# Stick-breaking attention: the first 512 keys of each unit multiplied on GpSimd and turned by TensorE in the score bank, the later keys by DMA

## The chip, the cores and the metric

The kernel runs on one core of one Trainium2 chip. The metric is device time in microseconds (us), from the first to the last instruction of one execution, as the median of several runs. Five engines work side by side, each through its own queue in order: TensorE (PE; its weight loads are shown as PEld), VectorE (DVE), ScalarE (ACT), GpSimd (POOL) and SyncE (SP), which here issues nearly all transfers to the DMA engines. SBUF is the working memory of 128 partitions; PSUM holds the matmul results in banks of 128 x 512 float32.

## What is computed

One layer of a streaming encoder with two kinds of attention heads side by side, on 2048 positions of width 1024. Cut to what matters here, the stick-breaking half:

```python
def one_block(args):                      # 128 queries of 8 heads, width 64
    qb, blk = args
    q_pos = blk * QBLK + jnp.arange(QBLK)
    z = jnp.einsum('bqhd,bkhd->bhqk', qb, k) * scale
    mask = (k_pos[None, :] < q_pos[:, None])[None, None]
    log_1mb = jnp.where(mask, jax.nn.log_sigmoid(-z), 0.0)
    rem = lax.cumsum(log_1mb, axis=3, reverse=True) - log_1mb
    a = jnp.where(mask, jnp.exp(jax.nn.log_sigmoid(z) + rem), 0.0)
    return jnp.einsum('bhqk,bkhd->bqhd', a, v)
```

So the weight of a key is sigmoid(z) times the product of sigmoid(-z) over the keys between it and the query. Ahead of it stand an RMS norm and one projection to q, k, v of both kinds of heads; behind it the output projection, a second norm and a gated feed-forward part.

## The kernel before

**Stages.** There are 8 groups of heads: groups 0 to 3 are one differential head each, groups 4 to 7 two stick-breaking heads each (`m` is 0 or 1). While a group's attention runs, the projection of the next group is woven in; under group 7 the output projection is woven in instead. The feed-forward part follows and takes the second half of the time. The order in each engine's queue is set when the kernel is built: the code yields work in pieces, a scheduler places the instructions by priorities (`PRI`) and its own costs, and `tc.issue_after(x)` keeps an instruction behind another one. On the chip each queue then runs in that order and waits where it must.

**A unit of stick-breaking** is one block `i` of 128 queries, one head `m` and up to 1024 keys (`b` counts these from the last); a group has 48 of them. `stage_a` treats a unit in chunks of 512 keys, the later chunk (`c` = 1) first, then `c` = 0. A group has 48 chunks with `c` = 0 and 32 with `c` = 1, 80 in all. For a chunk:

- TensorE makes the scores into a PSUM bank `sc` (`score_chunk`, L507; three products in half precision with high and low halves for groups 4 to 6, where `turned(g)` is true, and two for group 7). Four such banks go round in turn, so a chunk's bank is wanted again four chunks later.
- ScalarE makes sigmoid(-z) into `om` (L619) and sigmoid(z) (L620). VectorE's scan (L622) turns `om` into running products, from the last key to the first.
- The product of sigmoid(z) and the shifted `om` goes into `be` (L623). For groups 4 to 6 the chunk `c` = 1 has its sigmoid(z) in SBUF and GpSimd multiplies; every other chunk has it in the score bank and VectorE multiplies. With that the bank is free.

When both chunks are done, `split_t` splits the unit's whole `be` into high and low half-precision parts in `s16` (named `s` in profiles): the high part by a cast on ScalarE (L89), the low part by a subtraction on GpSimd (L98). One DMA transpose of SyncE (L461) turns both into `aT`, with the keys on the partitions. `PD` + 2 = 7 units later (group 7: 5), `stage_b` has TensorE multiply `aT` with the values (`pv`, L518), and `finish` normalizes a row of blocks; its four transposes are L489. `aT` has 6 buffers, and every fourth unit of groups 4 and 5 takes a spare one of another pool. L342 and L326 are the projections, L832 the output projection, L665 and L683/L684 the transposes of the inputs and their split.

Other numbers: `note` and `pick` keep tallies of each engine's load, by which some casts and subtractions choose an engine.

Of the kernel before, what the change touches and what calls it, by code (L numbers as in the profile page):

```python
# [11 lines left out]
F32 = mybir.dt.float32  # L12
# [26 lines left out]
QB, KB, ZB, AB, SB, PD = 4, 7, 9, 6, 3, 5  # L39
XL = (0, 4, 5, 1, 2, 6, 3)  # L40
# [19 lines left out]
def block(tc, a, out):  # L60
# [3 lines left out]
    with top:  # L64
# [192 lines left out]
        with ExitStack() as ph1:  # L257
# [254 lines left out]
            @pri("pv")  # L512
            def pv(G, yp, y0, aT, b, n, o, wd, start, stop):
                nb = n // P
                for j in range(nb):
                    v = G["v"][2 * b + j // 4][:, j % 4, :]
                    for q, (a_, v_) in enumerate(((j, o), (j, o + wd), (nb + j, o))):
                        PE.matmul(yp[:, y0 : y0 + wd], lhsT=aT[:, a_, :], rhs=v[:, v_ : v_ + wd], start=start and j == 0 and q == 0, stop=stop and j == nb - 1 and q == 2, skip_group_check=True)  # L518
# [77 lines left out]
            def sb_attn(g, G):  # L596
                last = {}
                front = []
                wide = [0]
                lag = PD + 2 if g < NG - 2 else PD  # L600

                @pri("at")
                def stage_a(i, m, b):
# [7 lines left out]
                    last[m] = om  # L611
                    for c in range((n - 1) // 512, -1, -1):
# [4 lines left out]
                        aside = c == 1 and turned(g)  # L617
                        beta = be[:, lo:hi] if aside else sc[:, :w]
# [4 lines left out]
                        (POOL if aside else DVE).tensor_tensor(be[:, lo:hi], beta, om[:, lo + 1 : hi + 1], ALU.mult)  # L623
                        note("A", 1.7 * w + 400)
                        note("D", 2.1 * w + 150)
                        note("P" if aside else "D", (1.65 if aside else 1.05) * w + 100)
                    wide[0] += 1
                    return n, split_t(be[:, :n], n, "A", "P", wide[0] if g < NG - 2 else None)
# [3 lines left out]
                def stage_b(i, m, b, n, aT):  # L632
                    with tc.issue_after(front[-1]):
                        stage_c(i, m, b, n, aT)

                def stage_c(i, m, b, n, aT):
# [4 lines left out]
                    pv(G, yp, P * r + 64 * m, aT, b, n, 128 * m, 64, r == 0 and m == 0 and b == i // 8, r == k - 1 and m == 1 and b == 0)  # L641
# [6 lines left out]
                for i in range(NT):  # L648
                    if i % 4 == 0:
                        level()  # L650
                    for b in range(i // 8, -1, -1):
                        for m in range(2):
                            n, aT = stage_a(i, m, b)
                            pend.append((i, m, b, n, aT))
# [3 lines left out]
                            yield done / (272 + 48 * CS), (i + 1 if b == 0 and m == 1 else i)  # L658
                for u in pend:
# [686 lines left out]
```

## Time and profile before

| | us |
|---|---|
| median of 3 runs | 2679.14 (2677.55 to 2685.42) |
| the profiled execution | 2680.8 |
| busy: TensorE | 2492.4 |
| busy: VectorE | 1932.7 |
| busy: GpSimd | 1489.1 |
| busy: ScalarE | 1347.0 |
| scans of stick-breaking, first and last start | 603.7 and 1353.3 |

The profile is one execution, taken by the hardware profiler; its span is 2680.8 us. A line such as `L622 DVE TENSOR_TENSOR_SCAN z<-z,sc 128x512 ... x168 | 213.5, 1274 | 13.5 <-ACT sc L620 6.0` reads: line 622, on VectorE, writes a tile `z` from `z` and `sc`, 168 times, 213.5 us in all, 1274 ns each on average; before these the engine idled 13.5 us, and 6.0 of that ended when ScalarE's line 620 was done. A line of waits gives the sum, the number and the longest. A line of a stretch gives its busy time for each engine, with the number of instructions, the granted TensorE clock (1.00 is full), the DMA share and rate. Groups that are cut by the edge of a stretch can differ by a call or two from the counts in the code. `om` and `be` are both named `z`.

### The profile page before, as it was taken

The page shows a single profiled execution, that of the slowest core. Times are in us where ns is not written, and L with a number is a line of the kernel's source. Part 1 is how long each engine was busy: PE and PEld are TensorE (multiplying, and loading weights), DVE is VectorE, ACT ScalarE, POOL GpSimd, SP SyncE. Part 2 cuts the span into 40 slices and gives each one's busy share as a digit, 9 for nine tenths or more (in the row PEclk, how much of TensorE's full clock was granted, in tenths as well). Part 3 has the DMA queues.
Part 4 walks back from the last instruction along what each step waited for, and adds up shares of the span by engine and source line. Part 5 has one row for each costly group of instructions (what it writes and reads, how often), then busy time and mean ns, then how long its engine had stood idle before and what let it go on. Part 6 is the DMA issues. An engine that isn't in the chain of part 4 may idle for free. (4 is left out here: it accounts for less than half of the span.)

```text
span 2680.8 us, 50579 instructions
## 1 busy us (share of the span) xinstructions
PE 2492.4 (93%) x19628; PEld 1498.6 (56%) x19628; DVE 1932.7 (72%) x3711; ACT 1347.0 (50%) x2487; POOL 1489.1 (56%) x1098
## 2 busy tenths in 40 slices
PE   6998989888988989889989899999999999999999
PEld 4655656577776776557775344444444444444444
DVE  6898969898989989877766868777685544444434
ACT  4665656567978878665644535344352112111121
POOL 2578667667767766546764656565564232322323
PEclk9999999999999999999999899999999999999999
DMA  6777697767998979987897574665649743635532
GB/s 222 213 162 181 146 200 168 179 143 184 193 179 179 185 160 209 210 191 217 218 285 282 208 250 178 255 226 202 245 183 346 293 177 143 233 141 186 195 111 95
DMA packets 619585, 534.41 MB, mean 199 GB/s; under 512 B 480640, under 2 KB 548224, under 8 KB 609104
## 3 DMA queue, kind: packets, MB, share of 16 engines
q1 hardware_dynamic: 617520, 529.09, 69.9%
q8 instruction: 154, 2.52, 0.4%
q0 software_dynamic: 512, 1.36, 0.2%
q14 instruction: 87, 0.71, 0.1%
q10 hardware_dynamic: 1312, 0.72, 0.1%
HBM read 261.08 MB, written 147.32 MB: 152 GB/s over the span
## 5 line engine op out<-in xcount | busy, mean ns | idle before, releaser
L98 POOL TENSOR_TENSOR s<-z,s 128x1024 f16<-128x1024 f32 (+7 forms) x288 | 472.0, 1647 | 142.5 <-ACT s L89 109.8
L507 PE MATMUL sc<-kT,qT 128*128 128x512 f16 (+3 forms) x1520 | 382.0, 353 | 53.3 <-DVE z L623 19.3
L622 DVE TENSOR_TENSOR_SCAN z<-z,sc 128x512 f32<-128x512 f32 (+3 forms) x320 | 352.8, 1112 | 58.6 <-ACT sc L620 38.0
L1138 PE MATMUL pd<-wd,act 128*128 128x512 f16 x1764 | 390.9, 379 | 1.2 <-DVE cg L1071 1.2
L326 PE MATMUL pj<-w,xt 128*128 128x384 f16 x1920 | 352.2, 331 | 18.8 <-ACT xt L683 6.9
L1030 PEld LDWEIGHTS <-wg 128*128 128x128 f16 x1848 | 182.0, 99 | 230.2 <-issue 16.4
L518 PE MATMUL yp<-v,aT 128*128 128x64 f16 (+1 forms) x4896 | 269.8, 204 | 41.6 <-DMA aT<-s 40.2
L518 PEld LDWEIGHTS <-aT 128*128 128x128 f16 x4896 | 237.5, 99 | 120.4 <-DMA aT<-s 52.5
L1030 PEld LDWEIGHTS <-wu 128*128 128x128 f16 x1848 | 180.7, 98 | 218.0 <-issue 2.6
L98 POOL TENSOR_TENSOR act<-cg,act 128x512 f16<-128x512 f32 x112 | 148.5, 1337 | 262.9 <-ACT act L1097 150.8
L1138 PEld LDWEIGHTS <-act 128*128 128x128 f16 x1764 | 172.8, 98 | 209.4 <-issue 2.8
L326 PEld LDWEIGHTS <-xt 128*128 128x128 f16 x1920 | 187.3, 99 | 147.5 <-issue 21.4
L89 ACT CAST s<-z 128x128 f16<-128x128 f32 (+7 forms) x215 | 173.1, 809 | 134.1 <-DMA aT<-s 40.5
L98 POOL TENSOR_TENSOR hs<-hs,cu 128x512 f32<-128x512 f32 x99 | 130.9, 1328 | 171.3 <-DVE hs L1144 70.8
L619 ACT ACTIVATE z<-sc,c 128x512 f32<-128x512 f32 (+3 forms) x320 | 210.7, 663 | 25.6 <-PE sc L507 11.7
L1097 ACT CAST act<-cg 128x512 f16<-128x512 f32 x126 | 77.3, 616 | 238.4 <-DVE cg L1103 162.7
L507 PEld LDWEIGHTS <-qT 128*128 128x128 f16 x1520 | 128.4, 99 | 121.0 <-DVE z L623 23.0
L832 PE MATMUL po<-wo,mt 128*128 128x256 f16 x1536 | 180.7, 277 | 13.9 <-DVE xf L835 8.4
L1030 PE MATMUL pm<-X,wu 128*128 128x512 f16 x792 | 180.4, 379 | 1.3 <-DVE wu L221 1.3
L1030 PE MATMUL pm<-X,wg 128*128 128x512 f16 x792 | 181.3, 382 | 0.0
L342 PE MATMUL pj<-xt,w 128*128 128x128 f16 x2304 | 175.0, 220 | 6.7 <-DVE v L364 5.7
L1144 DVE SCALAR_TENSOR_TENSOR hs<-pd,c,hs 128x512 f32<-128x512 f32 x136 | 99.0, 747 | 109.6 <-PE pd L1138 83.1
(266 smaller groups left out, 4737.6 us busy)
## 6 DMA issues: line engine op xcount, KB each, us to landing
xt<-xs SPq DMA_DIRECT2D x112, 512.0 KB, 4.3
hs<-hd SPq DMA_DIRECT2D x68, 512.0 KB, 4.5
hd<-hs SPq DMA_DIRECT2D x56, 512.0 KB, 4.7
split<-wg SPq DMA_DIRECT2D x11, 1792.0 KB, 7.8
split<-wu SPq DMA_DIRECT2D x11, 1792.0 KB, 6.7
split<-wd SPq DMA_DIRECT2D x11, 1792.0 KB, 7.2
wg<-split SPq DMA_DIRECT2D x11, 1792.0 KB, 7.3
wd<-split SPq DMA_DIRECT2D x11, 1792.0 KB, 12.2
```

Of the source, the lines that this page charges most:

```text
L89: ACT.copy(dst, src)
L98: (DVE if e == "D" else POOL).tensor_tensor(dst, a_, b_, op)
L326: PE.matmul(pj[:, :384], lhsT=xv[:, xi, kt, :], rhs=G["w"][:, wi, kt, :], start=n == 0, stop=n == 23)
L342: PE.matmul(o, lhsT=x_ if c == 2 else w_, rhs=w_ if c == 2 else x_, start=n == 0, stop=n == 23)
L507: last = PE.matmul(sc[:, : 128 * w].rearrange("p (t n) -> p t n", n=P), lhsT=G["q"][i // 4][:, a_, i % 4, :], rhs=G["k"][q][:, b_, 0:w, :] ...
L518: PE.matmul(yp[:, y0 : y0 + wd], lhsT=aT[:, a_, :], rhs=v[:, v_ : v_ + wd], start=start and j == 0 and q == 0, stop=stop and j == nb - 1 a ...
L619: ACT.activation(om[:, lo:hi], sc[:, :w], AF.Sigmoid, scale=G["nkz"][:])
L622: DVE.tensor_tensor_scan(ov, ov, sc[:, :w], om[:, hi : hi + 1], op0=ALU.mult, op1=ALU.bypass)
L832: PE.matmul(po[:, sl], lhsT=mt[:, kt, P * xi : P * xi + P], rhs=wos[2 * h + n][wi][:, kt, :], start=q == 0, stop=q == 23)
L1030: front[0] = PE.matmul(ps_[:].rearrange("p (t n) -> p t n", n=P), lhsT=wv[:, wo, wi, 128 * kt : 128 * kt + 128], rhs=X[xo][:, :, xi, kt, : ...
L1138: front[0] = PE.matmul(po[:], lhsT=act[:, ao, xi, 128 * j : 128 * j + 128], rhs=W["d"][:, wo, wi, :], start=start and u == 0 and q == 0, s ...
L1144: DVE.scalar_tensor_tensor(dst, po[:], kd[:], src, op0=ALU.mult, op1=ALU.add)
```

## The change

The chunk `c` = 0 takes another way, in all four groups:

- Its sigmoid(z) goes to SBUF, and GpSimd multiplies instead of VectorE. The chunk `c` = 1 is multiplied by VectorE out of the score bank, in groups 4 to 6 too.
- Its product is not sent through the DMA. Two chunks later (`TD` = 2) `turn_now` has TensorE transpose it block by block in float32, back into the chunk's own score bank; ScalarE casts from there into the high half of `aT`, and VectorE subtracts for the low half.
- The chunk `c` = 1 keeps the way by cast, subtraction on GpSimd and DMA transpose, alone and as soon as it is done, with half the size at most.
- `aT` is claimed at the start of a unit; `pv` gets a list of where each block lies in it. The value products come 5 units later in every group.

```diff
+TD = 2
@@ pv
-            def pv(G, yp, y0, aT, b, n, o, wd, start, stop):
+            def pv(G, yp, y0, aT, b, n, o, wd, start, stop, at=None):
                 nb = n // P
-                for j in range(nb):
+                at = at or [(j, nb + j) for j in range(nb)]
+                for j, (h_, l_) in enumerate(at):
@@ sb_attn
-                lag = PD + 2 if g < NG - 2 else PD
+                lag = PD
+
+                @pri("at")
+                def turn_now(sc, be, aT, nb):
+                    for j in range(nb):
+                        PE.transpose(sc[:, P * j : P * j + P], be[:, P * j : P * j + P], id32[:])
+                    hi, lo = (aT[:, o : o + nb, :].rearrange("p j n -> p (j n)") for o in (8, 8 + nb))
+                    ACT.copy(hi, sc[:, : P * nb])
+                    DVE.tensor_tensor(lo, sc[:, : P * nb], hi, ALU.subtract)
+                    note("A", 0.84 * P * nb + 110)
+                    note("D", 1.05 * P * nb + 70)
+
+                def turn_due(behind):
+                    while turns and turns[0][0] + behind <= len(front):
+                        with tc.issue_after(front[-1]):
+                            turn_now(*turns.pop(0)[1:])
@@ stage_a
+                    wide[0] += 1
+                    if n > 512 and g < NG - 2 and wide[0] % 4 == 3:
+                        aT = pp.tile([P, 4, 4, 2, 64], F16, tag="st", name=nm("aT"))[:].rearrange("p c t s e -> p (c t) (s e)")
+                    else:
+                        aT = sp.tile([P, 16, P], F16, tag="aT", bufs=AB, name=nm("aT"))
+                    at = {}
                     for c in range((n - 1) // 512, -1, -1):
...
-                        aside = c == 1 and turned(g)
-                        beta = be[:, lo:hi] if aside else sc[:, :w]
+                        turn_due(TD)
+                        beta = be[:, lo:hi] if c == 0 else sc[:, :w]
...
-                        (POOL if aside else DVE).tensor_tensor(be[:, lo:hi], beta, om[:, lo + 1 : hi + 1], ALU.mult)
+                        (POOL if c == 0 else DVE).tensor_tensor(be[:, lo:hi], beta, om[:, lo + 1 : hi + 1], ALU.mult)
...
-                    wide[0] += 1
-                    return n, split_t(be[:, :n], n, "A", "P", wide[0] if g < NG - 2 else None)
+                        if c == 0:
+                            turns.append((len(front), sc, be, aT, nb))
+                            continue
...
+                        to16(s16[:, :w], be[:, lo:hi], w, "A")
+                        tt(s16[:, w : 2 * w], be[:, lo:hi], s16[:, :w], ALU.subtract, w, "P")
+                        SP.dma_start_transpose(aT[:, : 2 * nb, :], s16[:, : 2 * w])
+                    return n, aT, [at[j] for j in range(n // P)]
...
+                turn_due(0)
                 for u in pend:
                     stage_b(*u)
```

The new kernel's lines are numbered on by up to 37. Three places show how the queues change. All lie in group 4, around the same unit, whose chunk `c` = 0 has the score bank `sc_10336` before and `sc_10493` now. First TensorE, before: a projection, the scores of that chunk, then value products of an older unit.

```order
L342 LDWEIGHTS xt_9984
L342 MATMUL pj_9833<-w_6485,xt_9984 128x128
L507 LDWEIGHTS qT_9395
L507 MATMUL sc_10336<-kT_8622,qT_9395 128x512
...
L518 LDWEIGHTS aT_9928
L518 MATMUL yp_9765<-v_7326,aT_9928 128x64
```

And now; `sc_10304` is the bank of the chunk four before `sc_10493`, so both are the same memory:

```order
L520 LDWEIGHTS aT_10045
L520 MATMUL yp_9689<-v_7963,aT_10045 128x64
L608 MATMUL sc_10304<-id_63,z_10288 128x128 x4
L508 LDWEIGHTS qT_9487
L508 MATMUL sc_10493<-kT_8620,qT_9487 128x512
```

The four transposes (L608) have moved in right ahead of the scores that reuse their bank.

VectorE around the same scans, before: a scan and a product for `c` = 0, a scan alone for `c` = 1 (`sc_10327`), and projection outputs between.

```order
L622 SCALAR_TENSOR_TENSOR z_10291<-z_10291,sc_10302 128x512
L622 SCALAR_TENSOR_TENSOR z_10325<-z_10325,sc_10327 128x128
L623 TENSOR_TENSOR z_10290<-sc_10302,z_10291 128x512
L610 COPY z_10456<-z_10291 128x1
L351 SCALAR_TENSOR_TENSOR qT_9395<-pj_9832,half_79,qT_9395 128x256
L363 TENSOR_SCALAR kT_9396<-pj_9832 128x256
L364 SCALAR_TENSOR_TENSOR kT_9396<-pj_9832,kT_9396 128x256
L622 SCALAR_TENSOR_TENSOR z_10325<-z_10325,sc_10336 128x512
```

And now (L646 is the scan, L647 the product, L611 the subtraction behind the transposes):

```order
L611 TENSOR_TENSOR aT_10246<-sc_10265,aT_10246 128x512
L646 SCALAR_TENSOR_TENSOR z_10422<-z_10422,sc_10438 128x512
L646 SCALAR_TENSOR_TENSOR z_10477<-z_10477,sc_10480 128x128
L611 TENSOR_TENSOR aT_10291<-sc_10304,aT_10291 128x512
L647 TENSOR_TENSOR z_10476<-sc_10480,z_10477 128x128
L628 COPY z_10602<-z_10422 128x1
L646 SCALAR_TENSOR_TENSOR z_10477<-z_10477,sc_10493 128x512
```

The product for `c` = 0 is gone; one for `c` = 1 and the subtraction, which waits for the transposes and the cast, have come.

GpSimd, before: products of `c` = 1 and subtractions of whole units.

```order
L623 TENSOR_TENSOR z_10290<-z_10290,z_10291 128x128
L98 TENSOR_TENSOR s_10149<-z_10130,s_10149 128x1024
L623 TENSOR_TENSOR z_10324<-z_10324,z_10325 128x128
L98 TENSOR_TENSOR s_10197<-z_10178,s_10197 128x1024
L98 TENSOR_TENSOR s_10310<-z_10290,s_10310 128x640
```

And now, products of `c` = 0 and subtractions of `c` = 1:

```order
L99 TENSOR_TENSOR s_10434<-z_10421,s_10434 128x128
L647 TENSOR_TENSOR z_10421<-z_10421,z_10422 128x512
L99 TENSOR_TENSOR s_10489<-z_10476,s_10489 128x128
L647 TENSOR_TENSOR z_10476<-z_10476,z_10477 128x512
L647 TENSOR_TENSOR z_10601<-z_10601,z_10602 128x512
L99 TENSOR_TENSOR s_10613<-z_10601,s_10613 128x512
```

The subtraction of `c` = 1 now stands ahead of the product of the same unit's `c` = 0, and its pieces have 512 keys at most.

24 lines of the change are left out of this document (16 added, 8 removed).

## The prediction

> **What bounds the kernel now.** I read the page first: span, busy shares, the 40 slices.
>
> ```profile
> span 2680.8 us, 50579 instructions
> PE 2492.4 (93%) x19628; PEld 1498.6 (56%) x19628; DVE 1932.7 (72%) x3711; ACT 1347.0 (50%) x2487; POOL 1489.1 (56%) x1098
> DVE  6898969898989989877766868777685544444434
> DMA  6777697767998979987897574665649743635532
> ```
>
> TensorE's 93% is an average in which the feed-forward part (from about 1400 us, DVE at 4 to 8 tenths) weighs most. The change lies in stick-breaking alone, so I asked next where that is: its scan (L622) runs nowhere else, and cutting the trace there gives each engine's load.
>
> ```profile
> L622 DVE TENSOR_TENSOR_SCAN z<-z,sc x320: 448/1270/1282, 603.7 to 1353.3; 128x512 f32<-128x512 f32 x91, 128x256 f32<-128x256 f32 x24, 128x384 f32<-128x384 f32 x24, 128x128 f32<-128x128 f32 x21
> ...
> core 0: us, PE busy (x) PEld busy (x) DVE busy (x) ACT busy (x) POOL busy (x), PEclk, DMA share, GB/s
> 604.00:1094.00 490.00, 437.03 (x6538) 344.76 (x6535) 442.91 (x769) 403.42 (x737) 357.53 (x268) 0.99 0.92 186
> 1094.00:1355.00 261.00, 229.64 (x2367) 178.46 (x2367) 203.79 (x356) 165.84 (x305) 146.73 (x101) 0.95 0.85 208
> ...
> 604.00:1094.00 490.00, 264.16 (x241) 0.99 0.92 186
> 1094.00:1355.00 261.00, 88.42 (x80) 0.95 0.85 208
> ```
>
> The last two rows are the scan alone: 240 of its 320 calls (groups 4 to 6, 80 each) fill 604 to 1094, group 7's 80 fill 1094 to 1355. In the first stretch VectorE is 90% busy, TensorE 89%, ScalarE 82%, GpSimd 73%, the DMA engines 92%. In the second TensorE leads with 88%, VectorE has 78%. To see whether VectorE's 10% idle is spread or lies in holes, I took its timeline in group 5:
>
> ```profile
> 908.07 0.69 DVE L623 TENSOR_TENSOR z<-sc,z 128x512 f32<-128x512 f32 x1
> 908.67 1.27 DVE L622 TENSOR_TENSOR_SCAN z<-z,sc 128x512 f32<-128x512 f32 x1
> 909.86 0.40 DVE L363 TENSOR_SCALAR v<-pj 128x256 f16<-128x256 f32 x1
> 910.29 0.43 DVE L364 SCALAR_TENSOR_TENSOR v<-pj,v 128x256 f16<-128x256 f32 x1
> 910.63 1.27 DVE L622 TENSOR_TENSOR_SCAN z<-z,sc 128x512 f32<-128x512 f32 x1
> 911.94 0.69 DVE L623 TENSOR_TENSOR z<-sc,z 128x512 f32<-128x512 f32 x1
> 912.55 0.14 DVE L610 COPY z<-z 128x1 f32<-128x1 f32 x1
> ```
>
> No row carries an idle bracket: one follows another, the pair of chunks taking two scans and one product. Where the pipeline runs, VectorE sets the pace; the idle lies in holes. So my ledger for groups 4 to 6 is VectorE's, and for group 7 TensorE's. The waits of 604 to 1094:
>
> ```profile
> ACT s L89 <- DMA aT<-s: 18.0, 11, 3.1
> PE yp L518 <- DMA aT<-s: 13.5, 12, 2.3
> DVE z L622 <- ACT sc L620: 13.3, 16, 3.4
> DVE z L622 <- ACT z L620: 12.9, 8, 4.0
> PE sc L507 <- DVE z L623: 12.4, 18, 1.6
> ```
>
> **The change part by part.** Per group there are 48 first chunks (c = 0) and 32 second ones (c = 1; 20 of 512 keys, 4 each of 384, 256, 128).
>
> *The product of c = 1, groups 4 to 6, moves from GpSimd to VectorE.* Today:
>
> ```profile
> L623 POOL TENSOR_TENSOR z<-z,z 128x512 f32<-128x512 f32 x60 | 68.1, 1135 | 46.4 <-DVE z L622 35.5 <-DVE z L608 6.0 <-DVE c L176 1.7
> L623 DVE TENSOR_TENSOR z<-sc,z 128x512 f32<-128x512 f32 x164 | 111.5, 682 | 3.3
> L623 DVE TENSOR_TENSOR z<-sc,z 128x384 f32<-128x384 f32 x20 | 11.1, 555 | 1.3 <-DVE z L622 0.5
> L623 DVE TENSOR_TENSOR z<-sc,z 128x256 f32<-128x256 f32 x20 | 8.4, 420 | 1.3 <-POOL s L98 0.5
> L623 DVE TENSOR_TENSOR z<-sc,z 128x128 f32<-128x128 f32 x12 | 3.4, 282 | 0.3
> ```
>
> On VectorE: 60 x 0.682 + 12 x (0.555 + 0.420 + 0.282) = 56 us. Records overlap a little: after a 0.69 product the next row starts 0.60 to 0.61 later (908.07 to 908.67, 911.94 to 912.55), so what it takes from the queue is 0.61 / 0.69 of that, 50 us. I take 50; it lies on the path of groups 4 to 6 in full, since 442.9 + 50 = 493 is more than their 490. GpSimd is relieved of 60 x 1.135 and the short ones; at 73% it gains nothing.
>
> *The product of c = 0 goes from VectorE to GpSimd, and its low half's subtraction from GpSimd to VectorE.* That swap is VectorE's, 48 calls each way per group. The nearest row for a subtraction out of PSUM into half precision is L684:
>
> ```profile
> L684 DVE TENSOR_TENSOR xt<-xtr,xt 128x512 f16<-128x512 f32 x32 | 21.1, 682 | 3.2 <-ACT xt L683 3.1
> L98 POOL TENSOR_TENSOR s<-z,s 128x1024 f16<-128x1024 f32 x120 | 266.1, 2221 | 57.0 <-ACT s L89 45.9 <-issue 6.0 <-DVE x L98 2.6
> ```
>
> 682 against 682 ns: nothing on VectorE. On GpSimd 2221 / 2 = 1110 out, 1135 in: nothing. Group 7 had all its products on VectorE, so the loss of c = 0's and the gain of its subtraction cancel there: 0.
>
> *TensorE turns c = 0:* 168 blocks of 128 x 128 a group, 504 in groups 4 to 6 and 168 in group 7.
>
> ```profile
> L665 PE MATMUL xtr<-id,z 128*128 128x128 f32 x224 | 33.1, 285 | 2.9 <-DVE z L229 2.1 <-DVE xt L684 0.8
> 1381.34 1.04 PE L665 MATMUL xtr<-id,z 128*128 128x128 f32 x8
> ```
>
> Eight end to end take 1.04 us, one alone 0.285, so each further one 0.11: 55 us and 18 us. The upper bound is 0.285 each (144 and 48 us), the lower is nothing, if all fall into idle time. In groups 4 to 6 TensorE comes to 437 + 55 = 492 of a stretch of 540 (91%): covered by VectorE's longer stretch, and the bill if that cover went is the 55. In group 7 it leads, so 18 count, less some of its own waits; I take 14.
>
> The Trainium skill, page "TensorE: Matmul & The Clock Gate", section "Part 4: PE-mode transpose", states about 275 ns for one (bf16, within a kernel). By it, an estimate, 504 of them would cost 139 us. The 1.04 us row disagrees for a run of eight, and I go by the row.
>
> *ScalarE:* a unit of 1024 keys needed one cast, it now needs two, one of them out of PSUM:
>
> ```profile
> L89 ACT CAST s<-z 128x1024 f16<-128x1024 f32 x83 | 89.3, 1077 | 59.3 <-DVE z L623 15.3 <-issue 14.3 <-DMA xcd<-x 7.9
> L89 ACT CAST s<-z 128x512 f16<-128x512 f32 x20 | 12.3, 624 | 12.7 <-DMA aT<-s 9.0 <-DVE y L487 2.3 <-POOL s L98 1.0
> L683 ACT CAST xt<-xtr 128x512 f16<-128x512 f32 x32 | 17.6, 587 | 6.7 <-PE xtr L665 6.1 <-ACT raw L375 0.5
> ```
>
> 624 + 587 - 1077 = 134 ns, 96 units in groups 4 to 6: 13 us on an engine with 87 idle. Nothing.
>
> *The DMA transposes* of stick-breaking fall from 192 to 128, each of at most 512 keys. SyncE gets 64 issues less, and its queue, in which projection loads stand behind them, waits less for GpSimd's subtractions. What can come back is the waits above: 13.5 us on TensorE, 18.0 on ScalarE. Neither is VectorE's, so I take 0; the far end is that VectorE's whole 47 us of holes go. The lag of 5 units instead of 7 works against it: a unit lasts 490 / 144 = 3.4 us, so a transpose has 17 us instead of 24 before its products are due. If those waits doubled, it costs another 13. The earlier claim of `aT` asks for no more buffers than lag and running unit, six.
>
> *The score bank is held longer.* A c = 0 bank was free after VectorE's product. Now the chain goes on: GpSimd's product (1.135 for 0.682), four transposes (0.285 + 3 x 0.11 = 0.6), the cast (0.587), the subtraction (0.682): 2.3 us more. Four banks go round, in 4 x 490 / 240 = 8.2 us. Today's chain for c = 0 is its scores (0.8), two sigmoids, scan and product:
>
> ```profile
> L619 ACT ACTIVATE z<-sc,c 128x512 f32<-128x512 f32 x224 | 162.2, 729 | 10.2 <-PE sc L507 9.4 <-DVE wo L221 0.5 <-PE sc L509 0.2
> L620 ACT ACTIVATE sc<-sc,c 128x512 f32<-128x512 f32 x164 | 115.2, 702 | 0.0
> 806.88 0.82 PE L507 MATMUL sc<-kT,qT 128*128 128x512 f16 x3 [0.90 <-DVE z L623]
> ```
>
> 0.8 + 0.73 + 0.70 + 1.27 + 0.68 = 4.2 without queues; with 2.3 it is 6.5, under 8.2 by 1.7. Between 0 and the second rival's price I take 0 beyond VectorE's term. The new waits are on TensorE (a transpose for GpSimd's product, the score four chunks on for the subtraction); behind both stand value products and projections, and everything downstream of those.
>
> **The sum.** 2680.8 + 50 + 14 = 2744.8 for the profiled execution. That one is 1.7 us above the median of the runs (2679.1), so 2743.
>
> **The rivals.** (1) *The holes take it.* Without DMA waits VectorE runs groups 4 to 6 at 100%: 493 for 490, +3, and group 7 hides part of the 18: +8. 2690. For it: aT waits are there to remove. Against: VectorE's waits name ScalarE, not a DMA.
>
> (2) *The bank decides.* In the new order many transposes stand close ahead of the score that reuses their bank. I priced the TensorE work between them by these rows and the score row:
>
> ```profile
> 799.64 0.72 PE L518 MATMUL yp<-v,aT 128*128 128x64 f16 x19
> 800.19 1.50 PE L342 MATMUL pj<-w,xt 128*128 128x128 f16 x24
> ```
>
> That is (0.72 - 0.19) / 18 = 0.03 us a value product, (1.50 - 0.22) / 23 = 0.056 a projection, 0.22 a score. About half of the 144 then have less than the 1.27 us of cast and subtraction, 0.5 on average: TensorE stands 72 x 0.75 = 54 us, and becomes the bound: 55 + 54 - 13.5 = +96; in group 7 a third are so placed, 18 + 12 = +30: 2805 by the median. It decides once queues add more than the 1.7 us of slack. For it: the bracket of 0.90 on the score row, and 12.4 us of such waits already.
>
> (3) *Transposes do not pipeline.* At 0.285 each TensorE has 437 + 144 = 581 in groups 4 to 6 (+91) and +48 in group 7, less 13.5 of waits: 2805. Against: the row of eight. The figure that the Trainium skill gives in its TensorE section, cited above, leads to about the same place.
>
> (4) *Faster: the DMA path is the governor.* With DMA share at 0.92, shorter chains let TensorE and VectorE run without holes. Groups 4 to 6 give +3; group 7's TensorE record holds run-outs (a burst's last matmul is booked long after the next could start), about 7%: 229.6 x 0.93 + 18 = 232, so 29 less than 261, if nothing else holds it. About half of that, 15, gives 2680.8 - 12 = 2669, 2667 by the median. It decides where group 7's holes are aT landings. Against, of group 7:
>
> ```profile
> L518 PE MATMUL yp<-v,aT 128*128 128x64 f16 x840 | 34.7, 196 | 1.9 <-DMA aT<-s 1.0 <-DVE mo L494 0.7
> ```
>
> Ahead of its value products TensorE idles 1.9 us in all, 1.0 of it for `aT`.
>
> The page "VectorE: DVE Perf Modes", section "The three transpose paths", speaks for this case: the Trainium skill gives 390 ns on TensorE against 1309 by DMA for one 128 x 128 tile, and advises TensorE. No run so far compares them; here the DMA's time lies on engines that nobody stands in line for, which a price per tile does not say.
>
> **How the numbers follow.** My forecast has 0.52 (own range 2715 to 2780), (1) 0.14, (2) 0.20, (3) 0.04, (4) 0.10. A change under 0.3% (8 us) can't be told from none. Slower: forecast, (2), (3) and about half of (1), 0.83; same: the rest of (1), 0.06; faster 0.11 with a little for what I don't see. The range goes from below (1), 2686, to above (2) and (3), 2812; it leaves out (4) and the tails.
>
> **What would show it.** Scans in groups 4 to 6 should spread over about 540 us, with VectorE above 90% there, product rows on VectorE by 96 calls more, the PSUM subtraction near 0.68 us, transposes adding about 73 us to TensorE, aT waits nearly gone. Rival 2 would show as TensorE idle ahead of scores, released by the subtraction, and VectorE below 90%. I am wrong if VectorE's busy time does not rise by about 50, or if the stretch shrinks in spite of it.

## The result, and the profile after

The changed kernel takes 2746.6 us (median of 4 runs, 2741.19 to 2749.4), the kernel before 2679.78 us (median of 4) on the same chip: a ratio of 1.0244, 95% interval 1.0227 to 1.0261. The forecast was 2743. The total came out; of its terms, two were mis-sized and one was missing.

The page of the changed kernel, its span, busy shares and the two rows of 40 slices that were shown of before:

```profile
span 2739.4 us, 52156 instructions
PE 2563.3 (94%) x20300; PEld 1572.1 (57%) x20300; DVE 1961.1 (72%) x3762; ACT 1372.8 (50%) x2655; POOL 1427.2 (52%) x1135
DVE  6898879888898988786765877786776544434434
DMA  6777687674445534564569565647657844635532
```

TensorE has 71 us more than before, VectorE 28, GpSimd 62 less, and in stick-breaking (the tenth slice to the twenty-first) the DMA engines fall from 7 to 9 tenths to 3 to 6. The scan (now L646), and the two stretches that it marks:

```profile
L646 DVE TENSOR_TENSOR_SCAN z<-z,sc x320: 452/1270/1282, 609.6 to 1413.7; 128x512 f32<-128x512 f32 x88, 128x128 f32<-128x128 f32 x24, 128x256 f32<-128x256 f32 x24, 128x384 f32<-128x384 f32 x24
...
core 0: us, PE busy (x) PEld busy (x) DVE busy (x) ACT busy (x) POOL busy (x), PEclk, DMA share, GB/s
610.00:1136.00 526.00, 486.63 (x6968) 393.83 (x6966) 466.42 (x825) 421.19 (x864) 275.10 (x264) 1.00 0.48 111
1136.00:1414.00 278.00, 244.71 (x2502) 196.63 (x2499) 203.77 (x344) 166.53 (x333) 156.29 (x138) 0.96 0.57 151
```

Cut at the first scan of group 4, the first of group 7 and the last of all, the two profiled executions differ like this:

| us | before | after | difference |
|---|---|---|---|
| up to the first scan of group 4 | 603.7 | 609.6 | +5.9 |
| groups 4 to 6 | 490.1 | 526.4 | +36.3 |
| group 7 | 259.5 | 277.7 | +18.2 |
| the rest | 1327.5 | 1325.7 | -1.8 |
| span | 2680.8 | 2739.4 | +58.6 |

The profiled execution of after is the fastest of its four runs (2741.19), with the highest mean granted clock (0.987, the others 0.982 to 0.984), so the table holds 58.6 of the 66.8 us between the medians. One execution against another says little about a few us in one stage whose order or granted clock differs. Where both are the same, a stage repeats well: groups 4 to 6 of e8 below, at a clock of 1.00 as here, take 526.4 us too.

VectorE was to be above 90% in groups 4 to 6; it is 466.4 / 526 = 88.7%, and TensorE, at 92.5%, is the fuller one. What waits there, in 610 to 1136 (line and what it waited for, sum, times, longest):

```profile
DVE z L646 <- ACT z L644: 26.3, 23, 5.1
ACT z L643 <- PE sc L510: 22.8, 24, 4.4
ACT z L643 <- PE sc L508: 20.7, 37, 1.6
PE sc L508 <- DVE aT L611: 13.5, 24, 1.3
DVE z L646 <- ACT sc L644: 13.2, 20, 1.7
PE sc L608 <- POOL z L647: 11.7, 17, 1.2
```

The chain reads backwards: the scan waits for ScalarE's sigmoids, and these (L643) wait for TensorE's scores. Of the waits shown of before, the two largest ended with a DMA's `aT`. They no longer stand among the waits, as the groups of after show (mean ns and idle time ahead behind the bars):

```profile
L508 PE MATMUL sc<-kT,qT 128*128 128x512 f16 x1064 | 305.3, 383 | 28.9 <-DVE aT L611 10.4 <-DVE z L647 4.7 <-DVE mx L549 3.8
L647 POOL TENSOR_TENSOR z<-z,z 128x512 f32<-128x512 f32 x144 | 160.5, 1115 | 236.0 <-DVE z L646 201.2 <-DVE xrs L156 6.6 <-DMA xt<-xs 6.2
L520 PE MATMUL yp<-v,aT 128*128 128x64 f16 x3264 | 139.2, 193 | 0.6 <-DMA aT<-s 0.3 <-ACT aT L610 0.3
L608 PE MATMUL sc<-id,z 128*128 128x128 f32 x672 | 110.3, 282 | 15.0 <-POOL z L647 14.0
L611 DVE TENSOR_TENSOR aT<-sc,aT 128x512 f16<-128x512 f32 x144 | 97.0, 675 | 12.7 <-ACT aT L610 12.3 <-ACT z L644 0.3
L610 ACT CAST aT<-sc 128x512 f16<-128x512 f32 x144 | 85.7, 598 | 6.3 <-PE sc L608 5.5
```

The value products of stick-breaking (L520 with 64 columns) wait 0.3 us for a DMA's `aT`. Those of 128 columns belong to groups 0 to 3, which the change leaves alone; they wait 22.8 us now and 26.4 before.

### The changeover to group 4

The first twenty microseconds of the stretch, and the rest of it, of before and then of after:

```profile
604.00:624.00 20.00, 19.45 (x301) 17.51 (x299) 17.26 (x37) 15.94 (x34) 16.09 (x12) 1.00 0.73 197
...
624.00:1094.00 470.00, 417.58 (x6241) 327.25 (x6238) 425.65 (x733) 387.48 (x705) 341.44 (x257) 0.99 0.93 185
```

```profile
610.00:630.00 20.00, 17.88 (x279) 16.26 (x277) 10.65 (x27) 9.22 (x29) 12.23 (x12) 1.00 0.67 169
...
630.00:1136.00 506.00, 468.75 (x6693) 377.58 (x6690) 455.77 (x799) 411.97 (x836) 262.87 (x252) 1.00 0.47 109
```

VectorE does 10.65 us of work in its first 20 instead of 17.26; from then on its share is the same in both kernels, 425.65 / 470 = 90.6% and 455.77 / 506 = 90.1%. The timeline of after has the place, VectorE first and then TensorE:

```profile
618.97 0.07 DVE L626 MEMSET z<- 128x1 f32 x2
624.14 1.01 DVE L646 TENSOR_TENSOR_SCAN z<-z,sc 128x384 f32<-128x384 f32 x1 [5.10 <-ACT z L644]
```

```profile
620.86 1.50 PE L520 MATMUL yp<-v,aT 128*128 128x128 f16 x24
622.25 0.65 PE L508 MATMUL sc<-kT,qT 128*128 128x384 f16 x3
```

VectorE stands 5.1 us for a sigmoid of 384 keys, whose scores come at 622.25; until then TensorE runs projections and value products of group 3. In before, the same engine had scores of that size at 609.11 and 616.02:

```profile
609.11 0.65 PE L507 MATMUL sc<-kT,qT 128*128 128x384 f16 x3
...
616.02 0.66 PE L507 MATMUL sc<-kT,qT 128*128 128x384 f16 x3
```

So in the new queue order group 4's scores of 384 keys stand further back. That is no accident of one execution. Over the profiles of this study the first scan of group 4 comes at 608 to 615 us in the eight kernels that turn `c` = 0 on TensorE (after and its variants) and at 599 to 606 in the six that don't; in the first 20 us VectorE works 10.1 to 13.6 us in the former and 16.7 to 17.3 in the latter. Why the scheduler put them there is open.

### The profile page after: what moved, and what is told of

It reads as the page before. It is cut to its first block, busy times and chain, and to the rows that moved or that the text cites. A ratio compares the mean times of both kernels' runs of the same rounds, so it can differ in the third digit from the quotient of the medians.

```text
span 2739.4 us, 52156 instructions
## 1 busy us (share of the span) xinstructions
PE 2563.3 (94%) x20300; PEld 1572.1 (57%) x20300; DVE 1961.1 (72%) x3762; ACT 1372.8 (50%) x2655; POOL 1427.2 (52%) x1135
## 4 chain that ended last, share of the span: by engine, by line
PE 38%; DVE 7%; issue 3%; POOL 1%; DMA 1%; ACT 1%; SPq 0%; DVEq 0%; POOLq 0%; ACTq 0%
PE pd L1175 14%; PE pm L1067 10%; PE pd L1067 6%; PE pa L1067 6%; DVE wd L222 1%; DVE wu L222 1%; PE po L869 1%; DVE cg L1140 1%; PE fsc L1000 0%; DVE cg L99 0%; DMA X<-xcd 0%; DVE act L99 0%; DVE z L646 0%; DMA xf<-in_x_dram 0%; POOL s L99 0%
## 5 line engine op out<-in xcount | busy, mean ns | idle before, releaser
L646 DVE TENSOR_TENSOR_SCAN z<-z,sc 128x512 f32<-128x512 f32 (+3 forms) x320 | 352.8, 1112 | 62.7 <-ACT z L644 37.5
L99 POOL TENSOR_TENSOR s<-z,s 128x1024 f16<-128x1024 f32 (+5 forms) x224 | 301.5, 1351 | 97.5 <-ACT s L90 93.5
L647 POOL TENSOR_TENSOR z<-z,z 128x512 f32<-128x512 f32 (+3 forms) x192 | 190.6, 996 | 267.2 <-DVE z L646 231.2
L520 PEld LDWEIGHTS <-aT 128*128 128x128 f16 x4896 | 236.4, 99 | 93.6 <-DMA aT<-s 31.4
L520 PE MATMUL yp<-v,aT 128*128 128x64 f16 (+1 forms) x4896 | 265.7, 203 | 23.7 <-DMA aT<-s 23.1
L643 ACT ACTIVATE z<-sc,c 128x512 f32<-128x512 f32 (+3 forms) x320 | 203.7, 637 | 60.7 <-PE sc L508 29.2
```

What stands on the lines that cost most here:

```text
L99: (DVE if e == "D" else POOL).tensor_tensor(dst, a_, b_, op)
L643: ACT.activation(om[:, lo:hi], sc[:, :w], AF.Sigmoid, scale=G["nkz"][:])
L646: DVE.tensor_tensor_scan(ov, ov, sc[:, :w], om[:, hi : hi + 1], op0=ALU.mult, op1=ALU.bypass)
L647: (POOL if c == 0 else DVE).tensor_tensor(be[:, lo:hi], beta, om[:, lo + 1 : hi + 1], ALU.mult)
```

## The experiments

Each ratio is to the kernel before, on the same chip, with its 95% interval; after stands at 1.0244. G4-6 and G7 are the lengths of groups 4 to 6 and of group 7 in that run's profile; shares are busy time over G4-6. The mean granted clock of a stretch differs between the runs, from 0.95 to 1.00 in G4-6 and from 0.93 to 1.00 in G7; where that bears on a reading, it is said.

| run | median us | ratio | G4-6 | TensorE | VectorE | G7 |
|---|---|---|---|---|---|---|
| before | 2679.78 | 1 | 490.1 | 89% | 90% | 259.5 |
| after | 2746.6 | 1.0244 (1.0227 to 1.0261) | 526.4 | 93% | 89% | 277.7 |
| e1 | 2725.52 | 1.0153 (1.0138 to 1.0168) | 515.0 | 93% | 82% | 275.2 |
| e2 | 2747.43 | 1.0236 (1.0217 to 1.0254) | 532.6 | 88% | 88% | 271.8 |
| e3 | 2731.3 | 1.0176 (1.0158 to 1.0194) | 517.6 | 94% | 85% | 272.9 |
| e4 | 2731.58 | 1.0175 (1.0160 to 1.0190) | 537.8 | 84% | 91% | 254.9 |
| e5 | 2763.94 | 1.0310 (1.0293 to 1.0326) | 574.2 | 88% | 78% | 257.7 |
| e6 | 2691.96 | 1.0043 (1.0028 to 1.0059) | 499.6 | 88% | 88% | 257.9 |
| e7 | 2749.78 | 1.0257 (1.0239 to 1.0276) | 533.6 | 91% | 89% | 274.8 |
| e8 | 2733.79 | 1.0192 (1.0175 to 1.0209) | 526.4 | 93% | 89% | 265.1 |
| e10 | 2740.71 | 1.0215 (1.0198 to 1.0233) | 537.9 | 91% | 87% | 265.6 |
| e11 | 2695.55 | 1.0054 (1.0035 to 1.0072) | 500.7 | 88% | 82% | 262.5 |
| e12 | 2671.67 | 0.9956 (0.9941 to 0.9971) | 489.6 | 87% | 90% | 248.8 |
| e13 | 2716.68 | 1.0123 (1.0103 to 1.0142) | 504.6 | 92% | 84% | 267.7 |

**e1: after, with the product of c = 1 back on GpSimd in groups 4 to 6.**

```diff
-beta = be[:, lo:hi] if c == 0 else sc[:, :w]
+beta = be[:, lo:hi] if c == 0 or turned(g) else sc[:, :w]
-(POOL if c == 0 else DVE).tensor_tensor(be[:, lo:hi], beta, ...)
+(POOL if c == 0 or turned(g) else DVE).tensor_tensor(be[:, lo:hi], beta, ...)
```

> The changed kernel, with the product of c = 1 back on GpSimd in groups 4 to 6, out of SBUF as before (52 us of VectorE's work there, 96 calls). Theory V, VectorE's added work sets the pace: 35 to 50 us faster than the changed kernel, near 2700 to 2710. Theory P, TensorE's transposes set it: no change, 2740 to 2750. Theory B, the longer hold of the score bank of c = 0 sets it: no change beyond 10, 2735 to 2750.

Measured: 0.9 percentage points, 24 us, come back, less than was expected with VectorE as the pace (35 to 50) and more than with TensorE or the banks. Its stretch, and what the scan waits for in it:

```profile
608.00:1123.00 515.00, 481.17 (x6948) 394.45 (x6946) 422.74 (x726) 416.16 (x863) 364.00 (x361) 0.99 0.51 115
...
DVE z L646 <- ACT z L644: 60.0, 82, 5.1
```

VectorE has 43.7 us less work than in after and the stretch is only 11.4 shorter: VectorE's scan now waits for this sigmoid of ScalarE 60 us instead of 26, and TensorE, at 481 of 515, has as little idle time as in after. So VectorE's product is not the whole price; without it some 25 us (515.0 - 490.1) stay in groups 4 to 6. The two profiled executions differ by 14.6 us, not 24: that of after is its fastest.

**e2: after, with half of each c = 0 chunk's transposes left out** (where it has an even number of blocks).

```diff
-for j in range(nb):
+h = nb if nb % 2 else nb // 2
+for j in range(h):
     PE.transpose(sc[:, P * j : P * j + P], be[:, P * j : P * j + P], id32[:])
...
```

The cast and the subtraction keep their size and read the first half twice.

> The changed kernel with half of the transposes left out in every first chunk of 256 or 512 keys; cast and subtraction read the transposed half twice, at full width (the attention output is wrong by that). 228 of 504 transposes go in groups 4 to 6 (25 us at 0.11) and 76 in group 7 (8 us). Theory V: only group 7's 8 come back, 2735 to 2742. Theory P: 33, near 2713. Theory B: the hold gets 0.22 shorter of some 8.8 us, about 10 of the 526 us, with group 7 2730.

```profile
611.00:1144.00 533.00, 471.01 (x6785) 374.14 (x6783) 468.07 (x828) 422.06 (x869) 276.57 (x266) 0.99 0.49 112
```

Measured: no change that can be told from after, though TensorE's busy time in groups 4 to 6 falls by 16 us, at a granted clock of 0.99 instead of 1.00. While VectorE has its full load, half of TensorE's transposes are covered there.

**e3: after, with the subtraction of c = 0 on half the columns.**

```diff
-DVE.tensor_tensor(lo, sc[:, : P * nb], hi, ALU.subtract)
+hb = P * ((nb + 1) // 2)
+DVE.tensor_tensor(lo[:, :hb], sc[:, :hb], hi[:, :hb], ALU.subtract)
...
-    at[4 * c + j] = (8 * (1 - c) + j, 8 * (1 - c) + nb + j)
+    at[4 * c + j] = (8 * (1 - c) + j, 8 * (1 - c) + nb + (j % ((nb + 1) // 2) if c == 0 else j))
```

> The changed kernel with the low half of c = 0 subtracted for half of the columns only, the value products reading that half twice (low halves of the other blocks are wrong). About 34 us of VectorE's work go in groups 4 to 6 and 11 in group 7; TensorE does the same. Theory V: 25 to 34 faster, 2713 to 2722. Theory P: no change, 2740 to 2750. Theory B: 0.3 us less of hold, 10 to 18 faster, 2730 to 2737.

```profile
615.00:1132.00 517.00, 484.10 (x6975) 394.29 (x6973) 438.74 (x819) 418.75 (x863) 274.02 (x264) 1.00 0.49 112
```

Measured: 0.7 percentage points, 18 us, come back. VectorE has 27.7 us less in groups 4 to 6, and the stretch is 8.8 shorter. As in e1, taking work from VectorE pays for a part of it only, and TensorE is then 94% busy. By the medians 2731.3 is what was expected if the bank's hold set the end (2730 to 2737); e7 speaks against that reading.

**e4: before, with the product of c = 1 on VectorE.** This is the first term of the prediction by itself.

```diff
-beta = be[:, lo:hi] if aside else sc[:, :w]
+beta = sc[:, :w]
-(POOL if aside else DVE).tensor_tensor(be[:, lo:hi], beta, ...)
+DVE.tensor_tensor(be[:, lo:hi], beta, ...)
```

> The kernel before with one part of the change alone: the product of c = 1 on VectorE out of the score bank in groups 4 to 6. Adds 50 us to VectorE there and nothing to TensorE. Theory V: 35 to 50 slower than before, 2715 to 2730. Theories P and B: within 10 of before, 2680 to 2690.

```profile
606.00:1143.00 537.00, 453.41 (x6572) 355.42 (x6570) 489.10 (x867) 405.26 (x736) 272.32 (x172) 0.96 0.83 170
```

VectorE gains 46 us of work and the stretch 47.7: about one for one, as priced, with VectorE at 91%. One thing is not parted from it: the mean granted clock is 0.96 here and 0.99 in before, and TensorE's busy time rises by 16.4 us though it has nothing more to do. By an estimate that takes all of the stretch to follow the clock, up to 0.03 x 537 = 16 us of the 47.7 go with it. The last section shows that the low clock follows TensorE's holes, so it may be VectorE's doing in turn.

**e5: before, with two more score products for each c = 0 chunk**: 72 us more for TensorE by the rows, 54 of them in groups 4 to 6.

```diff
+if more:                                  # more = (c == 0)
+    terms = terms + ((terms[1], terms[2]) if turned else (terms[0], terms[0]))
...
```

> The kernel before, with two of the score products of every c = 0 chunk made once more and added again (the scores are off by their low terms in groups 4 to 6, doubled in part in group 7). It gives TensorE the work of the transposes, 0.43 us for 512 keys, 54 us in groups 4 to 6 and 18 in group 7, without a longer use of the bank behind the product. Theory V (VectorE sets groups 4 to 6): 0 to 15 there and 10 to 18 in group 7, so 2695 to 2715. Theory P (TensorE): 50 and 18, near 2750. Theory B (banks): 0.43 of some 7.2 us of hold for 3 of 5 banks, 10 to 20, and group 7's 10 to 18, 2705 to 2715.

```profile
604.00:1178.00 574.00, 504.20 (x6866) 385.52 (x6863) 448.63 (x772) 409.25 (x740) 357.57 (x269) 0.95 0.77 160
```

TensorE's busy time rises by 67, the stretch by 84, and the run is slower than any of the three theories had it. The granted clock is 0.95: 574 x 0.04 = 23 us of the 84 would be the clock's, if all of the stretch followed it. So work put on TensorE in groups 4 to 6 of before is paid as well. This doesn't test the cover of the prediction, which was a stretch of 540 us: here 437 + 54 = 491 us fill before's whole 490. Group 7, with its 18 us, does not grow, but its granted clock is 0.99 for 0.95 in before, which could hide 0.04 x 258 = 10 of them.

**e6: before, with value products 5 units later instead of 7.**

```diff
-lag = PD + 2 if g < NG - 2 else PD
+lag = PD
```

> The kernel before, with the value products 5 units behind in groups 4 and 5 too, not 7. If the shorter lag costs anything where transposes go by DMA, 5 to 15 us: 2685 to 2700. All three theories of the changed kernel need nothing of it: 2675 to 2688.

```profile
PEld L518 <- DMA aT<-s: 34.0, 30, 3.1
PE yp L518 <- DMA aT<-s: 25.4, 25, 3.0
```

Where every unit goes by DMA, the shorter lag doubles TensorE's waits for `aT` (13.5 us before) and costs 0.43%, 9 to 12 us (granted clock 0.98 for 0.99). Only groups 4 and 5 had the lag of 7: the code has `PD + 2` for `g < NG - 2`, so group 6 had 5 all along, like group 7; the text ahead gives 5 for group 7 alone. The bound of 13 in the prediction was about right for this kernel; the changed one has hardly any such waits, so it doesn't pay that.

**e7: after, with the transposes into a newly claimed bank of the same pool**, so that `sc` comes free with GpSimd's product.

```diff
 def turn_now(sc, be, aT, nb):
+    sc = ps.tile([P, 512], F32, tag="sc", bufs=4, name=nm("tr"))
```

> The changed kernel, with the transposes of c = 0 written to a newly claimed score bank, so that the chunk's own is free after its scan and no bank waits for GpSimd's product and the two chunks of delay. The work on each engine stays the same. Theory B: 15 to 35 us faster than the changed kernel, 2715 to 2735. Theories V and P: no change, 2740 to 2752.

```profile
PEld tr L609 <- POOL z L648: 28.2, 38, 1.5
ACT aT L611 <- PE tr L609: 24.2, 25, 3.2
PE tr L609 <- POOL z L648: 22.5, 34, 1.3
```

Measured: nothing gained. The wait of scores for the subtraction no longer stands among the largest; instead the transposes stand longer for GpSimd's product, 22.5 us instead of 11.7. A shorter hold of the chunk's own bank (B in the expectations) brings nothing; about the same idle time of TensorE (22.5 for 13.5 + 11.7) shows at another instruction. The pool has four banks as before; no run gave it a fifth.

**e10: e7, with the transposes four chunks behind instead of two.**

```diff
-TD = 2
+TD = 4
```

> The changed kernel with the transposes four chunks behind their scores, not two, and in a bank of their own. Work per engine as in the changed kernel. A new theory, R: no engine and no bank is the limit of groups 4 to 6 now, but the round trip from a chunk's scores through ScalarE, VectorE's scan and GpSimd's product back to TensorE, which waits in order at the transpose two chunks later; with four chunks it fits, TensorE's idle ahead of transposes (22 us with banks of their own, 12 without) goes, and it is 15 to 30 us faster than the changed kernel, 2718 to 2735. If work is what counts (V or P): no change, 2740 to 2755.

```profile
PE tr L609 <- DVE z L647: 3.6, 8, 1.6
...
1151.00:1417.00 266.00, 238.71 (x2515) 193.77 (x2511) 200.39 (x345) 164.00 (x333) 152.21 (x137) 1.00 0.58 156
```

Measured: the largest sum of TensorE's waits ahead of the transposes falls from 22.5 us to 3.6, and groups 4 to 6 are no shorter (537.9). So the round trip over GpSimd (R) isn't shown as a limit there either. Group 7 is 12 us shorter than in after, which makes the run 0.3 points faster, with intervals that touch; its granted clock is 1.00 there for 0.96 in after, and 0.04 x 278 = 11 us would be that.

**e8: after, with group 7 multiplied on VectorE and sent by the DMA, chunk by chunk.**

```diff
+turn = c == 0 and g < NG - 1
-beta = be[:, lo:hi] if c == 0 else sc[:, :w]
+beta = be[:, lo:hi] if turn else sc[:, :w]
...
-(POOL if c == 0 else DVE).tensor_tensor(be[:, lo:hi], beta, ...)
+(POOL if turn else DVE).tensor_tensor(be[:, lo:hi], beta, ...)
...
-if c == 0:
+if turn:
     turns.append((len(front), sc, be, aT, nb))
...
-SP.dma_start_transpose(aT[:, : 2 * nb, :], s16[:, : 2 * w])
+o = 8 * (1 - c)
+SP.dma_start_transpose(aT[:, o : o + 2 * nb, :], s16[:, : 2 * w])
```

> The changed kernel, but group 7 multiplies on VectorE out of the bank and sends both chunks through cast, GpSimd's subtraction and the DMA, chunk by chunk; groups 4 to 6 as changed. If group 7's 18 us more are its 168 transposes on TensorE: 12 to 18 faster than the changed kernel, 2728 to 2738. If they come from elsewhere (the output projection woven in, the waits for x): no change, 2740 to 2750.

```profile
1137.00:1402.00 265.00, 220.74 (x2257) 171.43 (x2254) 197.99 (x344) 165.04 (x329) 146.70 (x129) 0.95 0.82 195
```

TensorE has 24 us less than in after's group 7, and the group is 12.6 shorter, two thirds of the 18.2, at about the same granted clock (0.95 for 0.96). So most of group 7's price is that of the way by TensorE; the run takes away cast, subtraction and GpSimd's product together with the transposes and doesn't part them.

**e11: before, with the c = 0 products of one head of two on GpSimd in groups 4 to 6**: 31 us off VectorE, no other change.

```diff
-aside = c == 1 and turned(g)
+aside = turned(g) and (c == 1 or m == 1)
```

> The kernel before, with the c = 0 product of the second head (m = 1) on GpSimd too in groups 4 to 6: 41 us less of VectorE, 70 more of GpSimd, which then has 427 of 490. It can beat both kernels. Theory V: 15 to 40 us faster than before, 2640 to 2665. If GpSimd's queue then delays casts and transposes, or TensorE is as near to the limit: within 10 of before, 2670 to 2690.

```profile
599.00:1100.00 501.00, 441.85 (x6550) 347.40 (x6548) 411.58 (x719) 404.51 (x731) 421.79 (x336) 0.98 0.90 181
...
PE yp L518 <- DMA aT<-s: 25.0, 25, 2.4
```

Slower by 0.5%. GpSimd rises to 421.79 of 501 (84%), and TensorE's waits for `aT` nearly double (25.0 for 13.5). In before, work added to VectorE is paid in full or nearly (e4), but work taken from it and given to GpSimd brings nothing. The run loads GpSimd as it relieves VectorE, so what the relief alone would bring stays open.

**e12: before, without the third score product of c = 0 in groups 4 to 6.**

```diff
+if less:                                  # less = turned(g) and c == 0
+    terms = terms[:2]
...
```

> The kernel before, without the third score product (query high times key low) of c = 0 in groups 4 to 6: 27 us of TensorE's work less there, the scores less exact. Theory V: within 8 of before, 2672 to 2688. If TensorE's work counts one for one in the kernel before, as its 54 us more did: 20 to 27 faster, 2653 to 2663.

```profile
603.00:1093.00 490.00, 424.09 (x6432) 342.32 (x6429) 440.56 (x777) 403.59 (x738) 356.20 (x267) 0.96 0.93 187
```

TensorE is 13 us less busy and the stretch keeps its 490. That speaks against TensorE alone as the limit of before, but weakly: the records of the scores cover 149 us instead of 172, 23 less, and the granted clock is 0.96 for 0.99, so up to 0.03 x 490 = 15 us may have been lost to it. The run is 0.44% faster all the same, in the profile from group 7 (248.8 for 259.5, at the same clock of 0.95), where nothing was left out; why is open. Such shifts, up to some 10 us in a stage whose work is the same but whose neighbour has changed, set how finely stages can be compared.

**e13: e1 and e2 together.**

> The changed kernel with both edits at once: the product of c = 1 back on GpSimd in groups 4 to 6 (44 us of VectorE) and half of the transposes left out (25 us of TensorE there, 8 in group 7; half of the turned weights are wrong). Alone the first gave back 24 us, the second nothing. Theory two, VectorE and TensorE are both near the limit in groups 4 to 6, so that either alone only uncovers the other: 35 to 50 us faster than the changed kernel, 2700 to 2712. Theory R, the round trip through the four engines' ordered queues is the limit, whatever the work: as the first edit alone or a little better by group 7, 2716 to 2728.

```profile
613.00:1118.00 505.00, 464.14 (x6756) 374.15 (x6753) 423.82 (x727) 418.23 (x867) 363.64 (x361) 0.98 0.50 117
```

Groups 4 to 6 fall to 504.6, another 10.4 below e1, for 17 us of TensorE's busy time; by the medians 0.3 points, with intervals that overlap by a little. Half of the transposes brought nothing with VectorE full (e2), and seem to bring something with VectorE relieved. That speaks for two engines near their limit that cover each other, but weakly: the median of 2716.7 misses the range of that theory (2700 to 2712) and lies at the near end of R's (2716 to 2728), which e10 spoke against. Neither theory is shown. 33 us above before remain: 9.8 of a later start (613.5 for 603.7), 14.5 in groups 4 to 6, 8.2 in group 7, in the profiles. The changeover, above, is in the first two.

## Why the prediction was right, and where it wasn't

**The direction.** The change relieves the DMA engines and GpSimd, which nobody waited for long, and loads VectorE and TensorE, both at about 90% in that stretch. That is what the ledgers said, and it agrees with what happened: GpSimd has 82 us less in groups 4 to 6, the DMA share goes from 0.92 to 0.48, and the time goes up. The fourth rival's premise came true (the value products of stick-breaking wait 0.3 us for `aT`), and no time was gained. The Trainium skill, page "VectorE: DVE Perf Modes", section "Rules for kernel authors", advises TensorE for a 128 x 128 transpose if PSUM will do as its destination. Here following it for `c` = 0, together with the other moves of this change, made the kernel 2.4% slower. In before, the time of the transposes by DMA lay mostly beside other work: TensorE's value products waited 13.5 us for them in groups 4 to 6. No run moved the transposes alone.

**VectorE's term: 50 forecast, 23.5 measured.** By the prediction's own test ("I am wrong if VectorE's busy time does not rise by about 50") this step failed in size. With each record counted only from where the one before it ended, the product of `c` = 1 brought 52.1 us, as priced. But the swap was not zero: 76.0 us of subtractions came in for 82.9 of products (675 ns for 682, and the rows overlap more). And 11.9 us of casts left VectorE that the diff doesn't touch: 43 casts of projection outputs before, 6 after. Of before, in 604 to 1094, and of after, in 610 to 1136:

```profile
L363 DVE TENSOR_SCALAR kT<-pj 128x256 f16<-128x256 f32 x20 | 8.3, 413 | 0.0
...
L363 DVE TENSOR_SCALAR v<-pj 128x256 f16<-128x256 f32 x15 | 6.1, 408 | 0.6 <-PE pj L342 0.5
```

```profile
L364 DVE TENSOR_SCALAR kT<-pj 128x256 f16<-128x256 f32 x5 | 2.1, 413 | 0.0
L364 DVE TENSOR_SCALAR v<-pj 128x128 f16<-128x128 f32 x1 | 0.3, 281 | 0.0
```

These casts choose VectorE or ScalarE by the load tallies of `note`; the change raised VectorE's tally, so they went to ScalarE (9 calls there before, 52 after, +12.1 us when counted the same way). The prediction had named the tallies and didn't follow them. The remaining 9.8 us less is spread over other lines. The sign "product rows on VectorE by 96 calls more" counted only one side as well: 96 of `c` = 1 came, 144 of `c` = 0 left.

**One for one, on the path.** e4 agrees with it for the term alone in the kernel before (46 of work, 47.7 of time, with the reservation on the clock). In the changed kernel it does not hold: there the same product, 43.7 us of VectorE's busy time, is worth 11.4 us of the stretch and 24 us by the medians (e1). The step that failed is that VectorE alone sets groups 4 to 6 after the change; it is 88.7% busy there and TensorE 92.5%, and relieving one shows the other. If one still prices the 23.5 at VectorE's old share of 0.904, they are 26 of the 36 us; that is arithmetic, and no run shows it.

**What was missing: the changeover**, 6.6 us less of VectorE's work in the first 20 us of group 4 (7 us of time at that share), and with the start 5.9 later about 13 us, an estimate from the two profiles. I priced no term for the order at a group's edge, and the order could have been read there.

**TensorE's term.** The size was good: 49.6 us more in groups 4 to 6 (55 forecast), 16.9 in group 7 (18), 71 on the page (73). These are net: counted like VectorE's records, the transposes take 63.4 us in groups 4 to 6 (500 records), and TensorE's other lines 14 less. By the 275 ns that the Trainium skill, page "TensorE: Matmul & The Clock Gate", section "Part 4: PE-mode transpose", gives for one, the 504 would have added 139, an estimate; the trace disagrees, since they go in runs (four in 0.61 us). The third rival fell with that. That they are covered, with a bill of 55 if the cover went, was right in kind: half of them are covered with VectorE full (e2), and about 25 us remain where VectorE is relieved (e1), not 55. That 25 also holds the changeover. Group 7 took 18.2 for my 14; e8 gives 12.6 of it back. These sizes move with the granted clock of the stretch: e10 gives back as much with all transposes in place, at 1.00 for 0.96.

**The bank, the second rival.** Its sign did show: VectorE below 90%, and scores that wait for the subtraction, 13.5 us and 24 times, as in this place:

```profile
802.94 0.61 PE L608 MATMUL sc<-id,z 128*128 128x128 f32 x4
804.88 0.81 PE L508 MATMUL sc<-kT,qT 128*128 128x512 f16 x3 [1.33 <-DVE aT L611]
```

But before had 12.4 us of such waits for VectorE's product, and transposes into a newly claimed bank gained nothing (e7). The working was also built on a mistake in the text ahead: it says that the banks go round in turn, and that `sc_10304` and `sc_10493` are the same memory. In the built program the banks don't come strictly in turn: the five score tiles from `sc_10304` to `sc_10493` lie in banks 2, 1, 0, 1 and 3. So the transposes that stand ahead of a score are not always those that it waits for.

**The lag of 5 units**: 0, as taken, with 1.0 us of TensorE's waits for `aT` left in 610 to 1136; e6 shows the 9 to 12 us that it costs where every unit goes by DMA.

**Together.** 50 + 14 = 64 was forecast, 36.3 + 18.2 + 5.9 - 1.8 = 58.6 measured in the profile. The VectorE term was about twice what it brought, and the missing changeover and TensorE's part made up for most of it. That the total came within 4 us was luck in good part.

**Open**: whether the swap of `c` = 0, its transposes or the longer round trip takes most of what e1 leaves; why the scores of group 4 moved back; what takes the 14.5 us in groups 4 to 6 that e13 still has over before beyond the changeover's share; and why group 7 got shorter in e12.

## What to carry to other kernels

Where several engines run near 90%, price a change by what it adds to each of them, and expect little from what it takes from one alone: relieving one of two seems to show the other (e1, e2, e13). Here work added to the fullest engine was paid about one for one (e4), but work taken from it was not earned back one for one (e1, e3). Where casts choose their engine by tallies, a changed tally moves work that the diff doesn't show, and the edge between two stages needs a term of its own. A hole that leaves TensorE mostly idle for 3.4 us costs clock behind it as well (last section).

## What the runs showed of the hardware

First, transposes of float32 on TensorE, each with a mean of 282 ns, cost little in a run: four take 0.61 us in the row at 802.94, so each further one (0.61 - 0.28) / 3 = 0.11, as the row of eight had let me forecast.

Second, the granted clock does not simply fall as TensorE's busy share rises. After had 1.00 in each of the 26 windows of 20 us from 610 to 1130, with TensorE 92.5% busy. Before had two lower ones of 25, and e5, 88% busy, 16 of 28 from 604 to 1164, two of its rows being these:

```profile
684.00:704.00 20.00, 20.00 (x257) 13.98 (x256) 18.05 (x29) 16.68 (x29) 15.78 (x11) 0.92 0.67 145
...
1084.00:1104.00 20.00, 15.70 (x200) 11.97 (x198) 13.30 (x22) 11.65 (x22) 9.76 (x8) 0.83 0.76 156
```

At this width the clock is low both where TensorE is busy throughout and where it has 4 us of holes. Cut finer, the records show what brings it down. In groups 4 to 6 of all 14 traces the clock is either full or half, and it changes at multiples of 3.41 us only; of such windows at full clock, those in which TensorE was busy for less than 40% were all followed by half clock (39 of 39), of those with 40 to 50% 10 of 27, of those with more none of 1978. So it is holes, not load, that bring the half clock, and what counts is the window before. The row of 684 to 704 above, in which TensorE is busy throughout, follows right on such a hole:

```profile
680.29:683.70 3.41, 1.11 (x5) 0.37 (x6) 3.41 (x7) 3.20 (x6) 0.44 (x2) 1.00 0.77 170
683.70:687.11 3.41, 3.41 (x16) 1.64 (x15) 2.92 (x5) 1.00 (x3) 3.41 (x3) 0.50 0.51 159
```

This makes the clock a part of what a wait costs. In e4 it happens while VectorE works throughout and TensorE not at all:

```profile
1005.60:1009.00 3.40, 0.00 (x0) 0.00 (x0) 3.40 (x7) 2.37 (x5) 1.71 (x1) 1.00 0.72 168
1009.00:1015.80 6.80, 5.06 (x25) 3.11 (x26) 4.50 (x20) 1.04 (x1) 4.26 (x4) 0.50 1.11 195
```

Where TensorE is held up like this, or perhaps where work taken from TensorE leaves holes (e12), half clock follows, and the next matmuls take longer. For a forecast it means that the mean clock of such a stretch can move by 0.04 with a change that names no such thing; where TensorE sets the pace, that would be, as an estimate, 0.04 x 526 = 21 us.
